# A reciprocal root in one ScalarE operation instead of two, and new paces for the streams of a two-layer trunk

## The chip, the cores and the metric

The kernel runs on one core of a Trainium2 chip. The metric is the device time of one execution in microseconds, the median of several runs.

## What is computed

The reference is a two-layer diffusion-transformer trunk in fp32: 512 latent tokens and 256 context tokens of width 1024. Cut to what matters here:

```python
def rmsnorm(x, g):
    xf = x.astype(jnp.float32)
    y = xf * lax.rsqrt(jnp.mean(xf * xf, axis=-1, keepdims=True) + EPS)
    return (y * g.astype(jnp.float32)).astype(x.dtype)
...
def modulate(x, shift, scale):
    return x * (1 + scale) + shift
...
def swiglu(h, w_gate, w_up, w_down):
    return (jax.nn.silu(h @ w_gate) * (h @ w_up)) @ w_down
```

Each layer is: modulated RMS norm, one input projection, two groups of heads side by side (a gated DeltaNet in both directions with a 64-token chunked triangular solve and a state scan, and multi-head latent attention with an RMS norm on its compressed queries and keys), one output projection, gated residual; then modulated RMS norm, SwiGLU feed-forward, gated residual. A final RMS norm ends it. EPS is 1e-6.

## The kernel before

Activations lie transposed, features on the 128 partitions and tokens along the free axis: a latent tile is 128x512, a context tile 128x256, and 8 of them make the width of 1024. Matrix products split each operand into a high and a low part and make three passes (`gemm`, L215 to L223; the matmul is L222). The helpers record every operation at their own line, so the same few lines recur in the trace: `tt` L140 (tensor with tensor on VectorE), `ts` L144 and L146 (with scalars), `stt` L149 (scalar and tensor), `act` L152 (any ScalarE operation).

**The RMS norm** is `rms_rows`. ScalarE squares the chunks, VectorE sums them, and TensorE adds over the partitions and spreads the sum over all of them (`pc`, L336, in PSUM). Then `q` is −0.5 times the mean plus EPS, `y` a first approximation of the reciprocal root, and one Newton step (Square, `tt`, `stt`) refines it. It is called 15 times: 8 of them 512 wide (latent, with the final one) and 7 of them 256 wide (context). `modulated` calls it ahead of the input projections and the feed-forwards, `mla_norm` for queries and keys, and the last lines of the kernel for the output. Behind it `modulated` scales and shifts eight chunks (VectorE L149, ScalarE into hx or m), and the next matmuls read these.

**The streams.** The program is written as 18 generators, the streams: `ctx_in`, `ctx_chain`, `ctx_mla`, `ctx_ffn`, `ctx_in1` for the context, `lat_in`, `lat_chain` (DeltaNet), `mla_prep`, `mla_att` (attention), `lat_ffn` for the latent tokens, `mod_rest` for the modulation vectors. Each yields now and then how much time it thinks its piece takes. `weave` keeps a clock of its own and always takes up the stream that is due first; a tie goes to the lower rank. The table TUNE gives each stream a rank and a pace, a factor on its yields. So the table decides the order in which the pieces are written into the program, and with it the order in every engine's queue; each engine works its queue off in order. Semaphores do the rest. In the chip no clock of `weave` exists.

Names that come up: the DeltaNet pre-stage (`gdn_pre`) solves 64x64 triangles with 62 small VectorE steps, transposes (L577, L578) and matmuls (L586, L587, L621); the scan's matmuls are L668, L680, L691; the output norm of a DeltaNet block takes its mean by L717, twelve small VectorE steps on 128x8 (`oq`, `ro0y` for the first block, `ro1y` for the second) and a spreading matmul L723. Attention finds row maxima in `prep` (products L932 and L937, reductions L933 and L938), sums in `attend` (L960 scores, L233 values and denominators) and divides by the denominator with the RECIPROCAL of L977. `Mod` multiplies the conditioning vector with the modulation weights (`wmod`, matmuls at L233 into psM, 24 units a layer), and its 256 KB loads go through SP's queue. PSUM tile rings: A has two buffers, M and F one each, B and C two.

Of the kernel before, what the change touches and what calls it, by code (L numbers as in the profile page):

```python
# [14 lines left out]
AF = mybir.ActivationFunctionType  # L15
# [14 lines left out]
EPS = 1e-6  # L30
# [3 lines left out]

C_ID, C_BLK1, C_TRIF, C_TRIB, C_SEL, C_MSK, C_ONE, C_BLKM, C_QB = 0, 128, 256, 384, 512, 520, 524, 525, 527
C_MIN = 529
NCONST = 657
B_MOD, N1, N2, CW, AL, DT, GN, QN, KN, FN = 0, 48, 56, 64, 124, 132, 140, 141, 143, 144
NSMALL = 152

# [9 lines left out]


TUNE = {
    ("ctx_in", 0): (3, 0.876),
    ("ctx_mla", 0): (3, 0.595),
    ("ctx_ffn", 0): (3, 0.702),
    ("ctx_in1", 0): (2, 1.0),
    ("ctx_chain", 0): (0, 0.7),
    ("mod_rest", 0): (1, 0.7),
    ("lat_in", 0): (2, 0.416),
    ("lat_chain", 0): (1, 1.0),  # L60
    ("mla_prep", 0): (4, 1.245),
    ("mla_att", 0): (5, 0.4),
    ("lat_ffn", 0): (6, 1.0),
    ("ctx_chain", 1): (2, 0.85),
    ("mod_rest", 1): (1, 1.0),
    ("lat_in", 1): (1, 0.7),
    ("lat_chain", 1): (0, 0.6),
    ("mla_prep", 1): (5, 1.755),
    ("mla_att", 1): (5, 1.07),
    ("lat_ffn", 1): (6, 1.0),  # L70
}

# [34 lines left out]
def trunk_kernel(ctx, tc, xin, cc, wmod, small, win, wuq, wuk, wuv, wout, wgu, wdn, cst, rope, out):  # L107
# [20 lines left out]
    def slot(tag, dt=F32, w=None):  # L128
        width = WIDTH[tag]
        t = sp.tile([P, width], dt, name=nm(tag), tag=tag, bufs=BUFS[tag])  # L130
        return t[:, 0:w or width]

    def ps(tag):
        return pp.tile([P, 512], F32, name=nm("ps" + tag), tag=tag, bufs=PSB[tag])
# [4 lines left out]
    def tt(out, a, b, op=ALU.mult, e=None):  # L139
        (e or V).tensor_tensor(out=out, in0=a, in1=b, op=op)  # L140

    def ts(out, a, s1, s2=None, op0=ALU.mult, op1=ALU.add, e=None):
        if s2 is None:
            (e or V).tensor_scalar(out=out, in0=a, scalar1=s1, scalar2=None, op0=op0)  # L144
        else:
            (e or V).tensor_scalar(out=out, in0=a, scalar1=s1, scalar2=s2, op0=op0, op1=op1)  # L146

    def stt(out, a, s, b, op0, op1):
        V.scalar_tensor_tensor(out=out, in0=a, scalar=s, in1=b, op0=op0, op1=op1)  # L149

    def act(out, a, f, **kw):
        A.activation(out, a, f, **kw)  # L152
# [7 lines left out]
    nc.sync.dma_start(out=cct, in_=cc)  # L160
    cst_t = cp.tile([P, NCONST], F32, name="cst")
    nc.sync.dma_start(out=cst_t, in_=cst)
# [160 lines left out]
    def rms_rows(st, chunks, scale, tag):  # L323
        n = st.n
        nk = len(chunks)
        pc = ps(tag)[:, 0:n]
        acc = None
        for k, c in enumerate(chunks):
            sq = slot(st.t, w=n)
            act(sq, c, AF.Square)  # L330
            if k and k < nk - 1:
                tt(acc, acc, sq, ADD)
            else:
                acc = sq
            if k >= nk - 2:
                PE.matmul(pc, ones_k.to_broadcast([P, P]), acc, start=k == max(nk - 2, 0), stop=k == nk - 1)  # L336
        q, y, t = (slot(st.t, w=n) for _ in range(3))
        ts(q, pc, -0.5 * scale, -0.5 * EPS)
        act(y, q, AF.Ln, scale=-2.0)
        act(y, y, AF.Exp, scale=-0.5)  # L340
        act(t, y, AF.Square)
        tt(t, t, q)
        stt(y, t, 1.5, y, ADD, MUL)
        return y

    def modulated(st, xs, al, modt, shift, tag, native=False):
        pr = rms_rows(st, xs, 1.0, tag)
        i = st.mi
        hs = []
        if native:  # L350
            for k in range(0, KD, 2):
                t = slot("m")
                for o in (0, 1):
                    h = t[:, NC_ * o:NC_ * o + NC_]
                    stt(h, xs[k + o], al[:, k + o, i:i + 1], pr, MUL, MUL)
                    act(h, h, AF.Identity, bias=modt[:, shift + k + o, i:i + 1])
                    hs.append(h)
            return hs
        for k in range(KD):
            t = slot(st.t, w=st.n)  # L360
            hi, lo = pair(st)
            stt(t, xs[k], al[:, k, i:i + 1], pr, MUL, MUL)
            act(hi, t, AF.Identity, bias=modt[:, shift + k, i:i + 1])
            stt(lo, t, modt[:, shift + k, i:i + 1], hi, ADD, SUB)
            hs.append((hi, lo))
        return hs
# [372 lines left out]
    def mla_norm(l, st, xs, scale, gn, tag):  # L739
        pr = rms_rows(st, xs, scale, tag)  # L740
        res = []
        for k, x_ in enumerate(xs):
            t = slot(st.t, w=st.n)
            stt(t, x_, smalls[l][:, gn + k:gn + k + 1], pr, MUL, MUL)
            if gn == KN and st is CTX:
                kc = sm([P, 2, NC_], "kvc", F32R)
                hi, lo = kc[:, 0, :], kc[:, 1, :]
            else:
                hi, lo = pair(st)
            split(t, hi, lo)  # L750
            res.append((hi, lo))
        return res
# [55 lines left out]
    scale = 96.0 ** -0.5  # L808
# [512 lines left out]
    weave([(TUNE[g.__name__, l][0], paced(g(*a), TUNE[g.__name__, l][1])) for g, l, a in todo])  # L1321
    xx = v.xx
    pr = rms_rows(LAT, xx, 1.0, "A")
    for k in range(KD):
        t = slot("t", w=NL)
# [33 lines left out]
def _constants():  # L1359
    f = np.float32  # L1360
    c = np.zeros((P, NCONST), f)
    p = np.arange(P)
    c[:, C_ID:C_ID + P] = np.eye(P, dtype=f)
    c[:, C_ONE] = 1.0 / D
    same = (p[:, None] // 64) == (p[None, :] // 64)
    c[:, C_BLKM] = (p < 64) / 64.0
    c[:, C_BLKM + 1] = (p >= 64) / 64.0
    c[:, C_BLK1:C_BLK1 + P] = same
    c[:, C_QB] = 64 * EPS * (p < 64)
    c[:, C_QB + 1] = 64 * EPS * (p >= 64)  # L1370
    c[:, C_TRIF:C_TRIF + P] = same & (p[:, None] <= p[None, :])
    c[:, C_TRIB:C_TRIB + P] = same & (p[:, None] >= p[None, :])
    for j in range(4):
        for r in range(2):
            c[32 * j + r, C_SEL + 2 * j + r] = 1.0
    first = (p // 32) % 2 == 0
    c[:, C_MSK] = first
    c[:, C_MSK + 1] = ~first
    c[:, C_MSK + 2] = -1.0 * first
    c[:, C_MSK + 3] = -1.0 * ~first  # L1380
    i = np.arange(64)
    for d, keep in enumerate((i[None, :] >= p[:, None] % 64, i[None, :] <= p[:, None] % 64)):
        c[:, C_MIN + 64 * d:C_MIN + 64 * d + 64] = np.where(keep, 3e38, -1e30)
    t = np.arange(NL)
    inv = f(10000.0) ** (-np.arange(0, 16, 2, dtype=f) / f(16))
    ang = []
    for pos in ((t // GRID_W).astype(f), (t % GRID_W).astype(f)):
        a = pos[:, None] * inv[None, :].astype(f)
        ang += [a, a]
    ang = np.concatenate(ang, axis=1).astype(f)  # L1390
    sign = np.where((np.arange(32) % 16) < 8, -1.0, 1.0).astype(f)
    rope = np.concatenate([np.tile(np.cos(ang).T.astype(f), (4, 1)), np.tile(np.sin(ang).T * sign[:, None], (4, 1))], axis=1)
    return c, rope
# [8 lines left out]
def _layout(i):  # L1402
# [19 lines left out]
    def heads(a):  # L1422
# [7 lines left out]
        [col(i["b_mod"], 48), col(i["norm1_g"], KD), col(i["norm2_g"], KD), cw, heads(i["a_log"]), heads(i["dt_bias"]),  # L1430
         gn, col(i["q_norm_g"], 2), col(i["kv_norm_g"], 1), fn], axis=2)
    o["cst"], o["rope"] = _constants()
    return {k: np.ascontiguousarray(v) for k, v in o.items()}

# [16 lines left out]
```

## Time and profile before

| | |
|---|---|
| median of 3 runs | 2228.44 us (2225.9 to 2229.92) |
| profiled execution, own time | 2224.78 us |
| its span (first to last instruction) | 2223.0 us |
| granted TensorE clock, mean | 0.946 |
| TensorE busy | 2032.2 us, 91% |
| VectorE busy | 1474.6 us, 66% |
| ScalarE busy | 889.5 us, 40% |
| loads of ScalarE tables | 41, 52.6 us |

All rows come from the profiled execution, which is 3.66 us below the median of the runs. The median holds 1.78 us more than the span in that execution (2224.78 less 2223.0). A share of busy time is a mean over stages with different limits; the windows in the section of rows take them apart. Granted clock is a share of TensorE's full speed, 1.00 being full.

### The profile page before, as it was taken

The page shows a single profiled execution, that of the slowest core. Times are in us where ns is not written, and L with a number is a line of the kernel's source. Part 1 is how long each engine was busy: PE and PEld are TensorE (multiplying, and loading weights), DVE is VectorE, ACT ScalarE, POOL GpSimd, SP SyncE. Part 2 cuts the span into 40 slices and gives each one's busy share as a digit, 9 for nine tenths or more (in the row PEclk, how much of TensorE's full clock was granted, in tenths as well). Part 3 has the DMA queues.
Part 4 walks back from the last instruction along what each step waited for, and adds up shares of the span by engine and source line. Part 5 has one row for each costly group of instructions (what it writes and reads, how often), then busy time and mean ns, then how long its engine had stood idle before and what let it go on. Part 6 is the DMA issues. An engine that isn't in the chain of part 4 may idle for free.

```text
span 2223.0 us, 40501 instructions
## 1 busy us (share of the span) xinstructions
PE 2032.2 (91%) x16048; PEld 1591.7 (72%) x16048; DVE 1474.6 (66%) x2904; ACT 889.5 (40%) x1583; POOL 69.6 (3%) x249
## 2 busy tenths in 40 slices
PE   5999988889998899899999998987976989999996
PEld 2876777789995557778888885765644677888885
DVE  4688668876689767769444457887687555444445
ACT  4445365444443534552323234534422234222233
POOL 0000001000000000000000000000000000000000
PEclk8999998899999999999999999996986999999998
DMA  8345514344446202242222236621110022233332
GB/s 327 136 155 188 172 32 124 112 143 132 127 155 208 85 11 80 93 146 91 86 76 96 89 113 221 190 78 29 44 34 11 30 76 76 95 99 96 96 99 76
DMA packets 130638, 240.48 MB, mean 108 GB/s; under 512 B 15185, under 2 KB 30065, under 8 KB 130449
## 3 DMA queue, kind: packets, MB, share of 16 engines
q1 hardware_dynamic: 124592, 224.16, 31.1%
q0 software_dynamic: 5856, 13.74, 2.3%
q8 instruction: 126, 2.06, 0.4%
q14 instruction: 64, 0.52, 0.1%
HBM read 228.30 MB, written 6.91 MB: 106 GB/s over the span
## 4 chain that ended last, share of the span: by engine, by line
PE 76%; DVE 10%; DMA 6%; ACT 5%; issue 3%; SPq 0%; POOL 0%; ACTq 0%; DVEq 0%; POOLq 0%
PE psA L222 35%; PE psM L222 14%; PE psF L222 4%; PE psB L960 3%; PE psA L233 2%; PE psA L227 2%; PE psB L621 2%; PE psM L233 2%; PE psC L668 1%; DVE fl L140 1%; DMA m<-wmod 1%; ACT t L152 1%; DVE g L140 1%; PE psC L680 1%; PE psC L691 1%
## 5 line engine op out<-in xcount | busy, mean ns | idle before, releaser
L222 PE MATMUL psA<-hx,wh 128*128 128x512 f32 x1680 | 537.0, 399 | 24.3 <-ACT hx L152 8.4
L152 ACT ACTIVATE wh<-wr 128x512 fp32r<-128x512 f32 (+2 forms) x410 | 249.1, 608 | 636.4 <-PE psA L222 466.6
L140 DVE TENSOR_TENSOR wl<-wr,wh 128x512 fp32r<-128x512 f32 (+2 forms) x410 | 269.5, 658 | 229.0 <-ACT wh L152 228.4
L222 PEld LDWEIGHTS psA<-hx,wh 128*128 128x128 f32 x1680 | 315.1, 190 | 113.7 <-issue 16.6
L222 PE MATMUL psA<-hx,wl 128*128 128x512 f32 x840 | 330.9, 394 | 1.3 <-DVE wl L140 1.3
L222 PE MATMUL psM<-hx,wh 128*128 128x512 f32 x704 | 217.4, 389 | 0.0
L222 PEld LDWEIGHTS psA<-hx,wl 128*128 128x128 f32 x840 | 159.4, 190 | 36.3 <-DVE wl L140 1.8
L152 ACT ACTIVATE fh<-fr 128x512 fp32r<-128x512 f32 (+3 forms) x186 | 110.7, 599 | 153.8 <-PE psF L222 45.5
L149 DVE SCALAR_TENSOR_TENSOR g<-psA,mod,g 128x512 f32<-128x512 f32 x112 | 83.9, 749 | 104.9 <-PE psA L222 104.6
L222 PEld LDWEIGHTS psM<-hx,wh 128*128 128x128 f32 x704 | 132.2, 188 | 27.2
L140 DVE TENSOR_TENSOR fl<-fr,fh 128x512 fp32r<-128x512 f32 (+3 forms) x186 | 120.0, 648 | 43.3 <-ACT fh L152 39.9
L222 PE MATMUL psM<-hx,wl 128*128 128x512 f32 x352 | 137.0, 389 | 0.0
L222 PE MATMUL psF<-m,fh 128*128 128x256 f32 x600 | 116.3, 292 | 7.1 <-ACT g L152 6.7
L222 PE MATMUL psA<-hd,wh 128*128 128x512 f32 x384 | 120.5, 392 | 0.0
L222 PEld LDWEIGHTS psF<-m,fh 128*128 128x128 f32 x600 | 95.6, 194 | 12.6 <-ACT g L152 9.1
L222 PE MATMUL psA<-ox,wh 128*128 128x512 f32 x320 | 100.7, 393 | 0.0
L222 PE MATMUL psM<-m,fh 128*128 128x256 f32 x416 | 82.1, 295 | 6.9 <-ACT m L152 5.7
L222 PE MATMUL psF<-m,fl 128*128 128x256 f32 x300 | 86.2, 287 | 2.2 <-DVE fl L140 2.1
L222 PEld LDWEIGHTS psA<-hd,wh 128*128 128x128 f32 x384 | 71.7, 188 | 16.4 <-DVE hd L140 1.1
L227 PE MATMUL psA<-m,g 128*128 128x256 f32 x320 | 75.3, 394 | 6.6 <-ACT m L152 3.4
L227 PEld LDWEIGHTS psA<-m,g 128*128 128x128 f32 x320 | 61.8, 197 | 20.3 <-ACT m L152 4.4
L222 PEld LDWEIGHTS psM<-hx,wl 128*128 128x128 f32 x352 | 66.0, 188 | 13.7
(382 smaller groups left out, 3643.0 us busy)
## 6 DMA issues: line engine op xcount, KB each, us to landing
wr<-wgu SPq DMA_DIRECT2D x176, 256.0 KB, 2.6
m<-wmod SPq DMA_DIRECT2D x160, 256.0 KB, 4.0
fr<-wgu SPq DMA_DIRECT2D x88, 256.0 KB, 2.7
wr<-win SPq DMA_DIRECT2D x80, 256.0 KB, 3.3
wr<-wdn SPq DMA_DIRECT2D x64, 256.0 KB, 2.6
g<-win SPq DMA_DIRECT2D x20, 512.0 KB, 6.3
g<-wmod SPq DMA_DIRECT2D x16, 512.0 KB, 10.2
fr<-wdn SPq DMA_DIRECT2D x32, 256.0 KB, 2.7
```

The costliest lines, as they stand in the source:

```text
L140: (e or V).tensor_tensor(out=out, in0=a, in1=b, op=op)
L149: V.scalar_tensor_tensor(out=out, in0=a, scalar=s, in1=b, op0=op0, op1=op1)
L152: A.activation(out, a, f, **kw)
L222: PE.matmul(o, ww[:, wk], xx if n is None else xx[:, a:a + n], start=cnt == 0, stop=cnt == 3 * nk - 1)
L227: PE.matmul(o, w[:, k * P:k * P + P], x_, start=k == 0, stop=k == len(xs) - 1)
L233: prev = mm()
L621: PE.matmul(pv[s, q, d, :], u3(lh[d])[s, c, :], u3(rh[d])[s, c, :], start=True, stop=True)
L668: PE.matmul(o[s], x_[s], y_[s], start=i == 0, stop=i == len(mm) - 1)
L680: PE.matmul(v4(ws)[s, hi, d, :], v4(w)[s, hi, d, :], S[s, hi, d, :], start=True, stop=True)
L691: PE.matmul(v4(kv)[s, hi, d, :], u3(ks[d])[s, unit(hi, n, d), :], v4(u)[s, hi, d, :], start=True, stop=True)
L960: PE.matmul(pst, K[ki][:, b:b + P], Q[qi], start=cnt == 0, stop=cnt == 2)
```

## The change

It has two parts. In `rms_rows` the logarithm and the exponential go, and one ScalarE function, Abs_reciprocal_sqrt, takes their place. It reads `pc` in PSUM directly, with the mean's factor as its scale and EPS as its bias, for which a column is added to the constants. The Newton step stays, and `q` for it too. And in TUNE 13 of 18 entries get other numbers.

```diff
-NCONST = 657
+C_EPS = 657
+NCONST = 658
...
 TUNE = {
-    ("ctx_in", 0): (3, 0.876),
-    ("ctx_mla", 0): (3, 0.595),
...
+    ("ctx_in", 0): (3, 0.815),
+    ("ctx_mla", 0): (0, 0.595),
...
-    ("mla_att", 1): (5, 1.07),
+    ("mla_att", 1): (5, 1.145),
...
         ts(q, pc, -0.5 * scale, -0.5 * EPS)
-        act(y, q, AF.Ln, scale=-2.0)
-        act(y, y, AF.Exp, scale=-0.5)
+        act(y, pc, AF.Abs_reciprocal_sqrt, bias=cst_t[:, C_EPS:C_EPS + 1], scale=scale)
         act(t, y, AF.Square)
         tt(t, t, q)
         stt(y, t, 1.5, y, ADD, MUL)
...
+    c[:, C_EPS] = EPS
```

The lines from the added one to the removed one stand one lower in the changed kernel (`act` is L153, `gemm`'s matmul L223, and so on); from L339 on they stand where they stood. Three places show what becomes of the queues. Loads of ScalarE's tables, which the kernel's text doesn't hold, appear in the order as ACT_TABLE_LOAD.

ScalarE at the end of the program, the final norm (g is the last residual chunk, psA the sum `pc`). Before:

```order
L152 ACTIVATE t_21204<-g_3265_18078 128x512 [waits DVE_49,Activation_49]
L152 ACT_TABLE_LOAD [waits DVE_49]
L152 ACTIVATE t_21208<-t_21207 128x512 [waits Activation_49]
L152 ACT_TABLE_LOAD
L152 ACTIVATE t_21208<-t_21208 128x512 [waits Activation_49]
L152 ACTIVATE t_21209<-t_21208 128x512 [waits PE_49,Activation_49]
```

After, the same place:

```order
L153 ACTIVATE t_21186<-g_3265_18065 128x512 [waits DVE_49,Activation_49]
L153 ACTIVATE t_21190<-g_3265_18065 128x512 [waits DVE_49,Activation_49]
L153 ACT_TABLE_LOAD [waits DVE_49]
L153 ACTIVATE t_21194<-psA_21168,cst 128x512 [waits Activation_49]
L153 ACTIVATE t_21195<-t_21194 128x512 [waits PE_49,Activation_49]
```

One load and one operation are gone; the load that is left waits for VectorE as the first load did.

VectorE at the end of the last triangular solve (small L140 steps on g and st) beside the last head pair's row maxima. Before:

```order
L140 TENSOR_TENSOR st_16899<-g_3095_16888,g_3096_16889 128x31
L140 TENSOR_TENSOR g_3096_16889<-g_3096_16889,st_16899 128x31
L577 STREAM_TRANSPOSE g_3094_16887<-g_3096_16889 128x32x32
L578 STREAM_TRANSPOSE g_3095_16888<-g_3096_16889 128x32x32
L933 TENSOR_REDUCE mx_17210<-psA_17211 128x1
...
L938 TENSOR_REDUCE mx_17210<-psA_17227 128x2
L140 TENSOR_TENSOR m_3175_17231<-mx_17210 128x4
L149 SCALAR_TENSOR_TENSOR g_3020_16504<-psB_17318,cst,g_3020_16504 128x16x32
```

After:

```order
L933 TENSOR_REDUCE mx_17189<-psA_17199 128x1
L141 TENSOR_TENSOR st_16964<-g_3119_16953,g_3120_16954 128x112
L141 TENSOR_TENSOR g_3120_16954<-g_3120_16954,st_16964 128x4x28
L938 TENSOR_REDUCE mx_17189<-psA_17202 128x2
L141 TENSOR_TENSOR st_16964<-g_3119_16953,g_3120_16954 128x87
L141 TENSOR_TENSOR g_3120_16954<-g_3120_16954,st_16964 128x3x29
L938 TENSOR_REDUCE mx_17189<-psA_17206 128x2
...
L141 TENSOR_TENSOR g_3120_16954<-g_3120_16954,st_16964 128x31
L577 STREAM_TRANSPOSE g_3118_16952<-g_3120_16954 128x32x32
L578 STREAM_TRANSPOSE g_3119_16953<-g_3120_16954 128x32x32
```

The six reductions (four L933, two L938) stood behind the transposes and now stand among the steps ahead of them.

VectorE and TensorE at the end of the second layer's attention and DeltaNet output (ro1 is the second block's chain, hx the split rows of the output projection). VectorE before:

```order
L140 TENSOR_TENSOR ro1t_17963<-ro1t_17963,oq_3229_17960 128x8
L977 RECIPROCAL t_18037<-psA_18034 128x512
L149 SCALAR_TENSOR_TENSOR ro1y_17962<-ro1t_17963,ro1y_17962 128x8
L149 SCALAR_TENSOR_TENSOR hd_17680<-t_18037,psA_17681 128x512
L140 TENSOR_TENSOR ro1t_17963<-ro1y_17962 128x8
```

VectorE after:

```order
L977 RECIPROCAL t_18024<-psA_18021 128x512
L141 TENSOR_TENSOR g_2742_14712<-g_2742_14712,psC_17590 128x256
L150 SCALAR_TENSOR_TENSOR hd_17610<-t_18024,psA_17611 128x512
L141 TENSOR_TENSOR g_2719_14594<-g_2719_14594,psC_17590 128x256
L141 TENSOR_TENSOR oq_3225_17852<-psC_17714,qe_16754 128x8
```

TensorE before:

```order
L717 MATMUL psC_17889<-cst,g_3021_16505 128x2 x4
L233 MATMUL psA_17681<-t_18028,m_15984 64x512
L233 MATMUL psA_17681<-t_18022,m_15984 64x512
L233 MATMUL psA_18034<-acc_17692,cst 64x512
L233 MATMUL psA_18034<-acc_17686,cst 64x512
L222 MATMUL psA_18104<-hx_18040,wh_18082 128x512
L222 MATMUL psA_18104<-hx_18041,wh_18082 128x512
L723 MATMUL psC_17889<-cst,ro1y_17962 64x128 x8
```

TensorE after:

```order
L717 MATMUL psC_17892<-cst,g_3025_16508 128x2 x4
L223 MATMUL psA_18129<-hx_18031,wl_18082 128x512
L223 MATMUL psA_18091<-hx_18035,wh_18069 128x512
L223 MATMUL psA_18129<-hx_18035,wh_18081 128x512
L223 MATMUL psA_18091<-hx_18036,wh_18069 128x512
L223 MATMUL psA_18091<-hx_18035,wl_18070 128x512
L223 MATMUL psA_18129<-hx_18036,wh_18081 128x512
L223 MATMUL psA_18129<-hx_18035,wl_18082 128x512
L723 MATMUL psC_17892<-cst,ro1y_17965 64x128 x8
```

The reciprocal moved ahead of the first block's chain (`oq` from psC), and output-projection matmuls of two columns (psA_18091, psA_18129) now stand around L717 and ahead of L723, where the attention's last matmuls stood before.

## Rows read from the trace of the kernel before

**Rows 1.** The page: busy time, share of the span and instructions.

```profile
PE 2032.2 (91%) x16048; PEld 1591.7 (72%) x16048; DVE 1474.6 (66%) x2904; ACT 889.5 (40%) x1583; POOL 69.6 (3%) x249
```

**Rows 2.** Windows: stretch, length, busy us of each engine, granted clock, DMA.

```profile
1495.00:1530.00 35.00, 23.45 (x517) 17.81 (x519) 26.08 (x42) 20.91 (x34) 0.52 (x1) 0.71 0.10 30
1530.00:1640.00 110.00, 93.28 (x1030) 64.06 (x1026) 81.88 (x184) 38.41 (x67) 9.69 (x25) 0.86 0.15 40
1640.00:1784.00 144.00, 113.22 (x1298) 69.45 (x1294) 101.31 (x207) 39.25 (x68) 1.95 (x4) 0.82 0.06 19
...
1850.00:2190.00 340.00, 340.00 (x1497) 279.93 (x1496) 155.25 (x235) 104.09 (x172) 0.00 (x0) 1.00 0.31 97
```

**Rows 3.** Timeline, the final norm: start, us, engine, line, operation.

```profile
2205.33 0.69 DVE L146 TENSOR_SCALAR t<-psA 128x512 f32<-128x512 f32 x1 [1.94 <-PE psA L336]
2206.10 1.28 ACT L152 ACT_TABLE_LOAD   x1 [1.99 <-DVE t L146]
2207.39 0.63 ACT L152 ACTIVATE t<-t 128x512 f32<-128x512 f32 x1
2208.04 1.28 ACT L152 ACT_TABLE_LOAD   x1
```

**Rows 4.** ScalarE's groups by shape: busy us, mean ns of one.

```profile
L152 ACT ACT_TABLE_LOAD x41 | 52.6, 1283 | 9.1 <-DVE t L146 6.0 <-DMA cct<-cc 2.5
...
L152 ACT ACTIVATE t<-t 128x512 f32<-128x512 f32 x33 | 20.7, 628 | 7.3 <-DVE t L149 4.7 <-DVE t L146 2.2
...
L152 ACT ACTIVATE g<-psA,small 128x512 f32<-128x512 f32 x18 | 12.2, 680 | 0.0
...
L152 ACT ACTIVATE tc<-tc 128x256 f32<-128x256 f32 x18 | 7.5, 416 | 2.3 <-DVE tc L146 2.1
```

**Rows 5.** Timeline, TensorE where it starts again behind four norms.

```profile
418.82 1.11 PE L222 MATMUL psM<-m,fh 128*128 128x256 f32 x2 [5.74 <-ACT m L152]
...
907.96 0.64 PE L376 MATMUL psB<-cst,m 32*64 32x16 f32 x16 [3.36 <-ACT m L152]
...
1500.46 0.23 PE L586 MATMUL psB<-g,g 32*32 32x32 f32 x1 [5.56 <-issue]
...
1839.31 0.79 PE L222 MATMUL psA<-hx,wh 128*128 128x512 f32 x1 [8.38 <-ACT hx L152]
```

**Rows 6.** Timeline, the second layer's input norm on ScalarE, and TensorE.

```profile
1349.09 1.39 ACT L152 ACTIVATE hx<-t,mod 128x512 fp32r<-128x512 f32 x2 [2.27 <-DVE t L149]
...
1351.03 1.94 PE L233 MATMUL psM<-m,sc 128*32 128x512 f32 x8 [1.96 <-DMA m<-wmod]
```

**Rows 7.** Timeline, the second layer's tail: VectorE's two chains, and TensorE.

```profile
1767.60 0.17 DVE L140 TENSOR_TENSOR oq<-psC,qe 128x8 f32<-128x8 f32 x1 [3.39 <-PE psC L717]
...
1769.68 0.17 DVE L149 SCALAR_TENSOR_TENSOR ro0y<-ro0t,ro0y 128x8 f32<-128x8 f32 x1
...
1774.52 0.17 DVE L140 TENSOR_TENSOR oq<-psC,qe 128x8 f32<-128x8 f32 x1 [2.01 <-PE psC L717]
...
1777.42 3.36 DVE L977 RECIPROCAL t<-psA 128x512 f32<-128x512 f32 x1
...
1781.81 0.17 DVE L149 SCALAR_TENSOR_TENSOR ro1y<-ro1t,ro1y 128x8 f32<-128x8 f32 x1
...
1780.83 1.22 PE L222 MATMUL psA<-hx,wh 128*128 128x512 f32 x2 [3.46 <-DVE ro1y L149]
```

**Rows 8.** Timeline, the first layer's tail, TensorE.

```profile
854.62 1.22 PE L222 MATMUL psA<-hx,wh 128*128 128x512 f32 x2 [1.21 <-DVE t L977]
```

**Rows 9.** Timeline, VectorE at the last row maxima.

```profile
1707.43 0.69 DVE L933 TENSOR_REDUCE mx<-psA 128x1 f32<-128x512 f32 x1 [1.18 <-PE psA L932]
...
1714.91 0.75 DVE L149 SCALAR_TENSOR_TENSOR g<-psB,cst,g 128x512 f32<-128x512 f32 x1
```

**Rows 10.** L233 in 687–726: matmuls (ns, first and last start), TensorE's idle (us, times).

```profile
L233 PE MATMUL psM<-m,sc x64: 592/605/617, 688.0 to 723.5; 128*32 128x512 f32 x64
...
  DMA m<-wmod: 3.5, 6
```

More of the change, by code (lines that the diff above doesn't have):

```diff
@@ L52 @@
 TUNE = {
-    ("ctx_in", 0): (3, 0.876),
-    ("ctx_mla", 0): (3, 0.595),
-    ("ctx_ffn", 0): (3, 0.702),
+    ("ctx_in", 0): (3, 0.815),
+    ("ctx_mla", 0): (0, 0.595),
+    ("ctx_ffn", 0): (3, 0.751),
     ("ctx_in1", 0): (2, 1.0),
-    ("ctx_chain", 0): (0, 0.7),
-    ("mod_rest", 0): (1, 0.7),
-    ("lat_in", 0): (2, 0.416),
+    ("ctx_chain", 0): (0, 0.651),
+    ("mod_rest", 0): (0, 0.49),
+    ("lat_in", 0): (3, 0.416),
     ("lat_chain", 0): (1, 1.0),
[L61 to L64, printed above, removed]
+    ("mla_prep", 0): (4, 1.332),
+    ("mla_att", 0): (4, 0.17),
+    ("lat_ffn", 0): (6, 0.911),
+    ("ctx_chain", 1): (2, 0.595),
     ("mod_rest", 1): (1, 1.0),
-    ("lat_in", 1): (1, 0.7),
-    ("lat_chain", 1): (0, 0.6),
+    ("lat_in", 1): (2, 0.7),
+    ("lat_chain", 1): (0, 0.642),
     ("mla_prep", 1): (5, 1.755),
-    ("mla_att", 1): (5, 1.07),
+    ("mla_att", 1): (5, 1.145),
     ("lat_ffn", 1): (6, 1.0),
```

## Prediction

> **What bounds the kernel now.** I read the page first, then the windows, then the waits and the timeline. TensorE is busy 2032 of 2223 us and ScalarE 890 [rows 1]: any gain has to come out of the 191 us in which TensorE waits (2223.0 − 2032.2), or out of the slower clock that follows a wait. The windows say where these lie [rows 2]. In 1850–2190, the second layer's feed-forward, TensorE is busy all of the time at a granted clock of 1.00: nothing that ScalarE or an order does there helps. The second layer's latent stage is different: 1495–1530 is busy 23.5 of 35 us at 0.71, 1530–1640 is 93.3 of 110 at 0.86, 1640–1784 is 113.2 of 144 at 0.82, 59 us of waiting in 289. There the chain alternates between TensorE and VectorE, and who stands in front of whom in a queue decides. So the ScalarE edit is priced where a norm stops TensorE, and the pace edit mainly here.
>
> **The ScalarE edit.** Before, a norm issues load, Ln, load, Exp; the final norm shows it: VectorE's scaling at 2205.33, load 2206.10, Ln 2207.39, load 2208.04 for 1.28, then Exp and Square [rows 3]. After, it is one load, one operation that reads PSUM with a pointer for its bias, and Square. The load stays, and so does its place: in the changed order the final load still waits for VectorE, since `ts(q, pc, …)` reads the same PSUM tile first and the new operation comes behind it. Saved are one load and one operation, less what PSUM and the pointer add. No row has this function. The nearest form, a 128x512 from PSUM with a pointer, has 680 ns, against 628 for `t<-t` [rows 4]; I take 680, since the rows show no operation of that shape that differs by its function (bounds 0.63, the plain row, to 1.28, as long as a load). Saving per 512-wide norm: 1.283 + 0.628 − 0.052 = **1.86 us**; per 256-wide norm, with 416 ns: 1.283 + 0.416 − 0.05 = **1.65 us**. For the upper bound of the operation it falls to 1.26.
>
> Fifteen norms have it, but few stand on the path. TensorE waits 8.38 us at the second feed-forward's norm, 3.36 at the second context norm (its gate copies queue behind the first latent feed-forward's norm on ScalarE), 5.74 at the context feed-forward's, 5.56 at the start of the second attention preparation [rows 5]. With the final norm, after which only output follows, that makes four of 512 (final, second feed-forward, first feed-forward, the key norm at 1493) and one of 256: 4 × 1.86 + 1.65 = **9.1 us**. The key norm is the weakest of these: its second load stands on ScalarE between two biased copies that the triangular solve's products wait for, so that without it the second copy comes earlier. Not counted is the second layer's input norm: there hx is ready at 1349.09, and TensorE then still waits 1.96 us for modulation weights until 1351.03 [rows 6]; the DMA is its cover, and without that it would be worth 1.86. The other nine lie beside other streams' matmuls (270–700, and 1340–1495), which is their cover; uncovered they'd be some 15 us more.
>
> The Trainium skill (ScalarE: Activation LUTs, "What ACT_TABLE_LOAD costs") gives a switch 1283 ns and a drain of about 1380 ns more. The trace agrees with the first (1283) and not with the second: Ln starts 0.01 us behind its load [rows 3]. By the page the five counted norms would save 5 × 1.38 = 6.9 us more; the sum goes by the row.
>
> What the edit adds: the new function's table stays, so the next Exp or Tanh on ScalarE needs a load that before was paid inside the norm. In the changed order I count 37 loads against 41, so of the 15 dropped 11 come back elsewhere (I find 12 places, the final norm needs none). They stand ahead of gate, softmax and SwiGLU operations; the one behind the second feed-forward's norm waits for that feed-forward's first matmuls, in a stretch where TensorE has no idle time [rows 2]. I cost them at nothing; each exposed one costs 1.28.
>
> **The pace edit** moves rows on all queues. Three places could be priced.
>
> *Second layer's tail.* The last DeltaNet outputs are normed by twelve small VectorE steps. Undisturbed, the first block takes from 1767.60 to 1769.85; the second takes from 1774.52 to 1781.98, because attention's last 3.36 us reciprocal and two sums stand among its steps, and TensorE's first output-projection matmul at 1780.83, which needs the PSUM tile that the reciprocal reads, waits 3.46 us [rows 7]. In the changed order reciprocal and scaling stand ahead of both chains, and 18 output-projection matmuls ahead of the last products. VectorE still has to do the reciprocal, so its 3.36 us move into the state scan; but TensorE has work then. At most the 3.46 wait and the half clock behind it go (about −6), at least nothing; I take **−3**. The first layer has the same in small, a wait of 1.21 for the reciprocal [rows 8]: **−1** (0 to −1.2).
>
> *Last row maxima.* Before, six reductions of the last head pair stand behind the two transposes of the triangular solve, and each waits about 0.9 us for TensorE, the first at 1707.43; the solve's next step is queued behind them and starts at 1714.91 [rows 9]. In the changed order they stand among the solve's 62 small steps, where their operands come in time or stop the solve. If their products are ready, 1707.43 to 1714.91 goes, plus the first, 9.2 us at most, but six of 0.69 us, 4.1 us, are put ahead of the transposes. Between −9.2 and +4.1 I take **−2**.
>
> Sum: −9.1 − 3 − 1 − 2 = **−15.1**, so the profiled execution of 2224.78 goes to 2209.7. The median shown is 2228.44, 3.7 above that execution, so I forecast **2213 us**.
>
> **Rivals.**
> *Larger gain.* The three places are those I could price, and other queues changed too: if a third of the 59 us in 1495–1784 goes instead of the 5 counted, that is 15 more, **2198**. For it: the clock there is 0.71 to 0.86, so a closed gap also speeds what follows. Against: the same streams with the same data, and VectorE busy most of that stretch, so that its chain can't shrink at will.
>
> *Nothing measurable.* Only norms with nothing beside them pay: final and second feed-forward, 3.7 us, and the orders cancel, **2225**. For it: nine of the fifteen are already covered, and the other three are read from waits that another late operand may end.
>
> *The loads come back on the path.* Twelve returning loads at 1.28 make 15.4 us and cancel the sum: **2228**. For it: they stand right ahead of softmax and gate exponentials, for which TensorE waits. Against: before, the second load of each norm was the same return, on a worse spot. The rule of the Trainium skill that bears on this is in ScalarE: Activation LUTs, "Table sets: the hidden batching unit": every change of set costs a load, and Ln and Exp share one set, so the old pair would need one load and the new function two. The trace differs, since the pair has two loads [rows 3]; that speaks against this rival.
>
> *Slower: a queue behind modulation weights.* Second-layer modulation products, eight groups at 687–724 with one weight transfer each, stand between the first attention's matmuls; they hardly wait now, 3.5 us in six times [rows 10]. In the changed order they stand elsewhere, several with only a few row-maximum products between two groups. TensorE's queue is in order: a group that comes up early stops attention until its transfer lands. The eight groups start 5 us apart (688.0 to 723.5 in seven steps), so one with nothing ahead of it costs up to 5.0. Three exposed take 15 and all of the gain; from four on (20, more than the 15.1 and the 4.5 of a measurable difference) the kernel is slower; with six, 30 − 15.1, it takes **2243**. Against: before, six waits made 3.5 us, 0.6 each, so the transfers keep up as long as attention's pace does.
>
> **How the numbers follow.** Main case 0.50, its own range 2204–2221 (the norms at 1.26 each, or the tail's bounds). Larger gain 0.23. Nothing measurable 0.09 and loads on the path 0.05, together 0.14 for within 0.2%, 4.5 us, about what a measurement here can tell from no change. Slower 0.13. Faster is 0.73. The range 2194–2232 holds the main case, most of the larger gain (below 2194 it would need over half of the 59 us, 0.08) and all without change; above lie the exposed groups, 0.10.
>
> **What would show it.** In the profile after: 37 loads; a final norm with one load and Square about 0.7 us behind the new operation's start, 1.9 us shorter; the wait at the second feed-forward's norm 6.5 instead of 8.4; the reciprocal ahead of the second block's chain, and no 3.5 us wait. The forecast is wrong if the new operation takes much over 0.7, if TensorE waits for modulation weights in the first attention, or if the row maxima stop the solve.

## The result and the profile after

The changed kernel takes 2211.35 us (2208.03 to 2213.97, 4 runs) against 2229.18 of before (4 runs): ratio 0.992, 95% interval [0.9904, 0.9936], that is 17.8 us less (14.3 to 21.4). The forecast was 2213. That it came so near is luck: two of its parts were far off and cancelled, as the experiments show. The ScalarE edit alone is worth 25 us, and the paces take some 7 of them back.

The page after, busy time by engine, as in [rows 1]:

```profile
PE 2033.4 (92%) x16048; PEld 1593.7 (72%) x16048; DVE 1473.7 (67%) x2904; ACT 877.0 (40%) x1564; POOL 69.5 (3%) x249
```

TensorE's work is the same and ScalarE's is 12.5 us less, 5.1 of it loads. ScalarE's groups by shape, which answer to [rows 4] (busy us, mean ns):

```profile
L153 ACT ACT_TABLE_LOAD x37 | 47.5, 1283 | 12.0 <-DVE t L147 6.0 <-DVE tc L147 2.8 <-DMA cct<-cc 2.4
...
L153 ACT ACTIVATE t<-psA,cst 128x512 f32<-128x512 f32 x7 | 4.8, 684 | 0.5 <-DVE t L147 0.5
L153 ACT ACTIVATE tc<-psF,cst 128x256 f32<-128x256 f32 x6 | 2.8, 471 | 3.1 <-DVE tc L147 3.0
```

The new function took 684 ns where 680 were taken. (Two more wide roots, which read psB, stand in a row of their own: the norm runs nine times 512 wide and six times 256 wide, not eight and seven times.) The final norm's timeline, for [rows 3]:

```profile
2195.85 0.69 DVE L147 TENSOR_SCALAR t<-psA 128x512 f32<-128x512 f32 x1 [1.94 <-PE psA L337]
2196.62 1.28 ACT L153 ACT_TABLE_LOAD   x1 [1.99 <-DVE t L147]
2197.92 0.69 ACT L153 ACTIVATE t<-psA,cst 128x512 f32<-128x512 f32 x1
2198.64 0.63 ACT L153 ACTIVATE t<-t 128x512 f32<-128x512 f32 x1
2199.30 0.69 DVE L141 TENSOR_TENSOR t<-t,t 128x512 f32<-128x512 f32 x1 [2.75 <-ACT t L153]
```

In the kernel before, the product behind Square started here:

```profile
2210.66 0.69 DVE L140 TENSOR_TENSOR t<-t,t 128x512 f32<-128x512 f32 x1 [4.64 <-ACT t L152]
```

From the start of VectorE's scaling to that of this product it is 3.45 us now (2199.30 less 2195.85) and was 5.33 (2210.66 less 2205.33): 1.88 less, where 1.86 was worked out. The new function starts 0.02 us behind its load's end, so here too the trace agrees with the 1283 ns of the Trainium skill (ScalarE: Activation LUTs, "What ACT_TABLE_LOAD costs") and shows none of the 1380 ns drain on top.

TensorE behind the four norms of [rows 5]:

```profile
414.06 1.13 PE L223 MATMUL psM<-m,fh 128*128 128x256 f32 x2 [5.38 <-ACT m L153]
...
902.57 0.65 PE L376 MATMUL psB<-cst,m 32*64 32x16 f32 x16 [1.48 <-ACT m L153]
...
1490.92 0.23 PE L586 MATMUL psB<-g,g 32*32 32x32 f32 x1 [7.12 <-issue]
...
1829.64 0.80 PE L223 MATMUL psA<-hx,wh 128*128 128x512 f32 x1 [6.50 <-ACT hx L153]
```

Two fell by 1.88 as forecast (8.38 to 6.50, 3.36 to 1.48). The context feed-forward's fell by 0.36, and the key norm's rose by 1.56. The end of the second transpose on VectorE (L578), first before, then in the changed kernel, shows what ended the key norm's wait:

```profile
1498.43 1.93 DVE L578 STREAM_TRANSPOSE g<-g 128x1024 f32<-128x1024 f32 x1
```

```profile
1488.89 1.93 DVE L578 STREAM_TRANSPOSE g<-g 128x1024 f32<-128x1024 f32 x1
```

In both traces the waiting products start 0.10 us behind that end (1500.46 behind 1500.36, 1490.92 behind 1490.82), so the norm was not what ended that wait. At the context feed-forward's norm it is the product behind Square on VectorE, first before, then in the changed kernel with Square ahead of it:

```profile
416.53 0.43 DVE L140 TENSOR_TENSOR tc<-tc,tc 128x256 f32<-128x256 f32 x1 [1.12 <-ACT tc L152]
```

```profile
409.91 0.42 ACT L153 ACTIVATE tc<-tc 128x256 f32<-128x256 f32 x1
...
411.75 0.42 DVE L141 TENSOR_TENSOR tc<-tc,tc 128x256 f32<-128x256 f32 x1
```

Before, VectorE waited for ScalarE here. Now Square ends at 410.33, and VectorE gets to the product 1.42 us later, since small steps of the triangular solve stand ahead of it: what ScalarE saved, the product waits in VectorE's queue.

The windows of the second layer's latent stage, for [rows 2] (same stages, the start of each found by the stage's first matmuls):

```profile
1482.80:1519.00 36.20, 23.77 (x465) 16.36 (x464) 27.07 (x48) 16.55 (x29) 0.52 (x1) 0.72 0.12 38
1519.00:1629.00 110.00, 97.05 (x1089) 66.96 (x1085) 86.36 (x190) 43.08 (x75) 9.48 (x25) 0.91 0.16 42
1629.00:1776.70 147.70, 113.37 (x1305) 69.87 (x1304) 98.56 (x204) 37.48 (x64) 1.95 (x4) 0.82 0.06 17
```

The three stages last 293.9 us; before, from 1494.0 to 1784.0, 290.0. Before, a group of modulation products stood between the latent input and the stage's start at 1494; counted from the last matmul of the latent input, with 2851 matmuls in both, it is 293.8 and 292.9. Here the forecast took 6.9 off (key norm, tail, row maxima); on equal work the profile shows 0.9 more. The tail, for [rows 7]:

```profile
1756.84 3.36 DVE L977 RECIPROCAL t<-psA 128x512 f32<-128x512 f32 x1 [0.37 <-PE psA L234]
...
1772.78 0.17 DVE L141 TENSOR_TENSOR oq<-psC,qe 128x8 f32<-128x8 f32 x1 [2.17 <-PE psC L717]
...
1775.34 0.17 DVE L150 SCALAR_TENSOR_TENSOR ro1y<-ro1t,ro1y 128x8 f32<-128x8 f32 x1
...
1760.26 0.73 PE L223 MATMUL psA<-hx,wh 128*128 128x512 f32 x2 [2.03 <-DVE t L977]
...
1775.56 1.09 PE L723 MATMUL psC<-cst,ro1y 128*64 128x128 f32 x16 [0.77 <-DVE ro1y L150]
1778.89 1.23 PE L223 MATMUL psA<-hx,wh 128*128 128x512 f32 x3 [2.24 <-ACT hx L153]
```

What was said of the order came true. The second block's chain takes 2.7 us instead of 7.5. But the reciprocal now delays the state scan ahead of it (2.03), and the output projection, which has started early, comes to the rows of the second block 2.24 too soon: 5.0 us of waits in place of 4.3 (3.46 and one of 0.87). The first layer's tail, for [rows 8], does the same in small: the wait for the reciprocal (1.21) is gone, and one for the second block's rows stands there:

```profile
854.87 1.55 PE L223 MATMUL psA<-hx,wh 128*128 128x512 f32 x3 [1.54 <-ACT hx L153]
```

The row maxima, for [rows 9]:

```profile
1689.72 0.69 DVE L933 TENSOR_REDUCE mx<-psA 128x1 f32<-128x512 f32 x1 [0.37 <-PE psA L932]
...
1697.62 0.69 DVE L938 TENSOR_REDUCE mx<-psA 128x2 f32<-128x512 f32 x1 [0.45 <-PE psA L937]
...
1699.18 1.92 DVE L577 STREAM_TRANSPOSE g<-g 128x1024 f32<-128x1024 f32 x1
```

Each of the six waits for its product, 0.26 to 0.45 (before, five of the six did, 0.89 to 1.18), now in front of the solve's last steps. The transpose behind the solve, in the kernel before:

```profile
1701.96 1.94 DVE L577 STREAM_TRANSPOSE g<-g 128x1024 f32<-128x1024 f32 x1
```

From the last matmul of the latent input to this transpose's end it was 212.8 us and is now 218.2 (1701.10 less 1482.9); from there to the last of L723 it was 80.1 and is 75.6. The stage lost ahead of the transposes what it won behind them.

At the first attention, TensorE's waits for modulation weights, for [rows 10] (us, times):

```profile
  DMA m<-wmod: 4.1, 3
```

The slower rival did not come: 3.5 us in six waits became 4.1 in three, the longest 2.62, and the stage as a whole got shorter. This table gives the last matmul of a stream in each trace, as its difference to before in us (the last line is the span); the runs are those of the next section.

| last matmul of | before | changed | ars_only | tune_only | five_norms | ten_norms | old_layer2 |
|---|---|---|---|---|---|---|---|
| latent input, layer 0 | 267.9 | −5.2 | −7.4 | +2.9 | −0.7 | −4.1 | −3.4 |
| context feed-forward | 684.7 | −0.6 | −7.0 | +10.5 | −1.3 | −4.5 | −4.3 |
| first attention | 851.2 | −9.3 | −7.9 | +1.5 | +1.5 | −7.7 | −14.4 |
| latent feed-forward, layer 0 | 1338.5 | −7.6 | −10.9 | +6.1 | −3.0 | −10.5 | −9.9 |
| latent input, layer 1 | 1491.1 | −8.2 | −10.8 | +7.3 | −2.7 | −11.2 | −11.0 |
| latent DeltaNet, layer 1 | 1784.0 | −7.3 | −10.4 | +10.7 | +1.3 | −7.4 | −15.1 |
| latent feed-forward, layer 1 | 2202.4 | −9.5 | −12.9 | +9.6 | −1.3 | −7.7 | −17.7 |
| span | 2223.0 | −11.1 | −14.8 | +9.4 | −3.2 | −7.6 | −19.8 |

A profiled execution is one draw. That of before lies 4 us under its median, that of `ars_only` 7 above its own, so the table places gains and losses between stages and is no measure of the sum. A second execution of `ars_only` (`root_only_again`, below) differs from the first by up to 2.7 us in it.

### The profile page after: what moved, and what is told of

It reads as the page before. It is cut to its first block, busy times and chain, and to the rows that moved or that the text cites. A ratio compares the mean times of both kernels' runs of the same rounds, so it can differ in the third digit from the quotient of the medians.

```text
span 2211.9 us, 40502 instructions
## 1 busy us (share of the span) xinstructions
PE 2033.4 (92%) x16048; PEld 1593.7 (72%) x16048; DVE 1473.7 (67%) x2904; ACT 877.0 (40%) x1564; POOL 69.5 (3%) x249
## 5 line engine op out<-in xcount | busy, mean ns | idle before, releaser
L223 PE MATMUL psA<-hx,wh 128*128 128x512 f32 x1680 | 541.0, 401 | 21.7 <-ACT hx L153 12.4
L153 ACT ACTIVATE wh<-wr 128x512 fp32r<-128x512 f32 (+2 forms) x410 | 248.9, 608 | 651.4 <-PE psA L223 462.2
L223 PEld LDWEIGHTS psA<-hx,wh 128*128 128x128 f32 x1680 | 317.6, 192 | 112.3 <-ACT hx L153 15.7
L223 PE MATMUL psA<-hx,wl 128*128 128x512 f32 x840 | 334.1, 398 | 0.0
L223 PE MATMUL psM<-hx,wh 128*128 128x512 f32 x704 | 218.2, 390 | 0.0
L223 PEld LDWEIGHTS psA<-hx,wl 128*128 128x128 f32 x840 | 161.1, 192 | 37.7 <-issue 0.8
L153 ACT ACTIVATE fh<-fr 128x512 fp32r<-128x512 f32 (+3 forms) x186 | 110.6, 600 | 148.1 <-PE psM L223 41.2
L223 PEld LDWEIGHTS psM<-hx,wh 128*128 128x128 f32 x704 | 132.6, 189 | 27.4
L223 PE MATMUL psM<-hx,wl 128*128 128x512 f32 x352 | 137.0, 389 | 0.0
L223 PE MATMUL psF<-m,fh 128*128 128x256 f32 x600 | 115.5, 291 | 7.5 <-ACT g L153 6.8
L223 PE MATMUL psA<-hd,wh 128*128 128x512 f32 x384 | 120.5, 392 | 0.0
L223 PEld LDWEIGHTS psF<-m,fh 128*128 128x128 f32 x600 | 94.8, 193 | 14.3 <-ACT g L153 8.3
L223 PE MATMUL psA<-ox,wh 128*128 128x512 f32 x320 | 100.7, 393 | 0.0
L223 PE MATMUL psF<-m,fl 128*128 128x256 f32 x300 | 85.9, 286 | 1.3 <-DVE fl L141 1.3
L223 PE MATMUL psM<-m,fh 128*128 128x256 f32 x416 | 81.2, 293 | 5.9 <-ACT m L153 5.4
L223 PEld LDWEIGHTS psA<-hd,wh 128*128 128x128 f32 x384 | 71.7, 188 | 16.5 <-DVE hd L141 1.1
L153 ACT ACTIVATE t<-psB 128x512 f32<-128x512 f32 x80 | 47.6, 597 | 72.5 <-PE psB L960 50.0
L223 PEld LDWEIGHTS psM<-hx,wl 128*128 128x128 f32 x352 | 66.2, 188 | 13.7
```

Of the source, the lines that this page charges most:

```text
L223: PE.matmul(o, ww[:, wk], xx if n is None else xx[:, a:a + n], start=cnt == 0, stop=cnt == 3 * nk - 1)
```

## The experiments

Theory A is the prediction's: five norms are on the path, and the order gives 6 us more. The rivals: B, that only the two norms with nothing beside them pay and the order does the rest; C, that the ten norms costed at nothing are paid for too. Medians in us; the ratio is to before, run beside each.

| run | median | ratio [95% interval] |
|---|---|---|
| the changed kernel | 2211.35 | 0.992 [0.9904, 0.9936] |
| ars_only | 2202.82 | 0.9888 [0.9872, 0.9905] |
| tune_only | 2232.5 | 1.0018 [1.0001, 1.0034] |
| root_first | 2210.41 | 0.9918 [0.9896, 0.994] |
| old_layer2 | 2207.14 | 0.9906 [0.9893, 0.9919] |
| five_norms | 2222.47 | 0.9972 [0.996, 0.9983] |
| ten_norms | 2217.18 | 0.9943 [0.993, 0.9955] |
| root_att0_paces | 2206.16 | 0.9885 [0.9869, 0.9901] |
| root_first_old_paces | 2195.09 | 0.9843 [0.9825, 0.986] |
| load_back | 2220.97 | 0.9953 [0.9935, 0.9971] |
| ctx_paces | 2206.91 | 0.9901 [0.9886, 0.9916] |
| no_newton | 2185.02 | 0.9804 [0.9788, 0.9821] |

**The two parts alone.** `ars_only` has the ScalarE edit and TUNE of before; `tune_only` the reverse, with logarithm and exponential:

```diff
-        act(y, q, AF.Ln, scale=-2.0)
-        act(y, y, AF.Exp, scale=-0.5)
+        act(y, pc, AF.Abs_reciprocal_sqrt, bias=cst_t[:, C_EPS:C_EPS + 1], scale=scale)
```

> Only the ScalarE edit; TUNE as before. Theory A (the prediction's terms): five norms on the path give 9.1 us, so about 2220 against 2229. Theory B (only norms with nothing beside them pay, that is the final one and the second feed-forward's, and the order does the rest): 3.7 us, about 2225.5. Both expect the final norm, from VectorE's scaling to the first output product, 1.9 us shorter.

> Only the pace edit; logarithm and exponential stay. Theory A: the order gives 6 us, so about 2223. Theory B: the order gives what theory B's norms don't, 17.8 - 3.7 = 14, so about 2215. If the two edits add up, this gain and that of the ScalarE edit alone make 17.8 us.

Both theories missed both. The ScalarE edit gives 25 us (21 to 29), the paces cost 4 (0.2 to 7.6). Added, −21 lies within the noise of the measured −17.8.

**Which norms.** `five_norms` has the new function where the prediction counted it and the old pair elsewhere; `ten_norms` is the counterpart. Each caller passes the flag `one`:

```diff
-        act(y, pc, AF.Abs_reciprocal_sqrt, bias=cst_t[:, C_EPS:C_EPS + 1], scale=scale)
+        if one:
+            act(y, pc, AF.Abs_reciprocal_sqrt, bias=cst_t[:, C_EPS:C_EPS + 1], scale=scale)
+        else:
+            act(y, q, AF.Ln, scale=-2.0)
+            act(y, y, AF.Exp, scale=-0.5)
```

> TUNE as before; the new function only in the five norms that the prediction counted (context feed-forward, both latent feed-forwards, the second layer's key norm, the final one), logarithm and exponential in the other ten. Theory A (the five carry the gain): 9.1 us off 2229, so 2220, and the ten carry the rest only through the order. Theory C (the other ten, most of them in the first 400 us, are on the path too): also about 2220, but then the ten alone give the missing 17 us.

> The counterpart: the new function only in the other ten norms, TUNE as before. Theory A: they lie beside other work, 2229 less 0 to 2. Theory C: 15 to 17 us less, 2212 to 2214; in the trace the first 270 us come out about 7 us shorter, as they did with all fifteen.

The five give 6.2 us (3.8 to 8.9), a little less than the 9.1. The ten give 12.7 (10.0 to 15.6), twice as much, and they were costed at nothing; theory C wanted 15 to 17. The table of stages says where the ten gain: 4.1 up to 268, 3.2 in the first attention, 2.8 in the feed-forward behind it; 3.8 are lost again between 1491 and 1784. Five and ten together make 18.9, some 6 less than the 25 of all fifteen; the intervals overlap, and no run says what those 6 are. ScalarE in the kernel before, in the stretch of the context's query and key norms:

```profile
189.47 0.68 ACT L152 ACTIVATE t<-psA,small 128x512 f32<-128x512 f32 x1
190.16 1.28 ACT L152 ACT_TABLE_LOAD   x1
191.46 0.42 ACT L152 ACTIVATE tc<-tc 128x256 f32<-128x256 f32 x1
191.78 0.62 ACT L152 ACTIVATE wh<-wr 128x512 fp32r<-128x512 f32 x1
192.42 1.28 ACT L152 ACT_TABLE_LOAD   x1
193.71 0.87 ACT L152 ACTIVATE tc<-tc 128x256 f32<-128x256 f32 x2
...
196.78 0.70 ACT L152 ACTIVATE tc<-m 128x256 f32<-128x256 f32 x2
...
197.23 1.13 PE L336 MATMUL psF<-tc,cst 128*128 128x256 f32 x4 [1.96 <-ACT tc L152]
```

and the same place in `ars_only`:

```profile
188.11 1.28 ACT L153 ACT_TABLE_LOAD   x1 [1.83 <-DVE t L150]
...
190.25 0.71 ACT L153 ACTIVATE tc<-m 128x256 f32<-128x256 f32 x2
...
190.71 1.13 PE L337 MATMUL psF<-tc,cst 128*128 128x256 f32 x4 [0.33 <-ACT tc L153]
```

ScalarE hardly idles here (15.99 of 18 us below), whatever its 40% over the span. A load doesn't only delay its own norm: the next norm's squares (tc<-m) and the weight splits (wh<-wr), on which other streams' matmuls wait, stand behind it in the one queue. Windows of 188 to 206, first before, then `ars_only`:

```profile
188.00:206.00 18.00, 16.05 (x77) 12.05 (x76) 15.36 (x33) 15.99 (x27) 0.71 (x3) 1.00 0.25 87
```

```profile
188.00:206.00 18.00, 17.67 (x88) 12.95 (x81) 16.96 (x38) 15.13 (x27) 1.71 (x7) 1.00 0.51 164
```

TensorE, busy 16.05 of 18 us before, gets 17.67. The windows are the same stretch of time and not quite the same work, since `ars_only` is some us ahead here; the wait of 1.96 that became 0.33 is the closer comparison.

**The load by itself.** `load_back` is `ars_only` with a 128x1 exponential behind the root, which brings the load back into the norm:

```diff
         act(y, pc, AF.Abs_reciprocal_sqrt, bias=cst_t[:, C_EPS:C_EPS + 1], scale=scale)
+        act(t[:, 0:1], y[:, 0:1], AF.Exp)
```

> The ScalarE edit with TUNE as before, and right behind the root a 128x1 exponential into a column that Square overwrites: it forces the table load that the edit took out of the norm, and little else. If the gain of 26 us is the load inside the norm (theory C, all fifteen norms count with 1.28 of their 1.7 to 1.9 us), most of it goes: 2203 + 15 x (1.28 + 0.2) = 2225 at most, 2218 to 2225. If it is the shorter chain of wide operations or the order alone that helped: 2203 to 2208.

18 us come back by the medians (14.5 by the ratios), of 25, some of it the added operation itself (201 ns, fifteen times). So the load in that place is likely most of the gain; it is not shown apart from the order, since over 270 of VectorE's 2904 instructions stand elsewhere in its queue than in `ars_only`. It is not a smaller count of loads: `ars_only` has 39 in its order, before 41, `load_back` 42. Thirteen of the fifteen loads that left the norms came back, ahead of gates and exponentials. They seem to cost little there: in the trace of `ars_only` one of them, at 899.3, is followed within 2.5 us by a wait of TensorE for ScalarE, of 0.85.

**The chain of the norm.** Two kernels shorten it with TUNE of before; the first issues the root ahead of VectorE's scaling, the second leaves out the Newton step too, and with it the scaling, so that its root is only as exact as the new function:

```diff
-        ts(q, pc, -0.5 * scale, -0.5 * EPS)
         act(y, pc, AF.Abs_reciprocal_sqrt, bias=cst_t[:, C_EPS:C_EPS + 1], scale=scale)
+        ts(q, pc, -0.5 * scale, -0.5 * EPS)
```

> The ScalarE edit with TUNE as before, and the root issued ahead of VectorE's scaling of the same tile. Theory A: 0.8 to 2.0 us for each exposed norm, for five norms 4 to 10 below 2203, so 2193 to 2199. If the scaling is hidden but at the second feed-forward and the final norm: 2199 to 2201.

> TUNE as before and the root first, but without the Newton step: scaling, Square, product and last step are left out, so the root is only as exact as the new function. On the final norm's chain that is 2.1 us (Square 0.63, product and step 0.69 each, gaps). Theory C (each of the fifteen norms is paid in full or nearly, as 24 to 28 us for fifteen times 1.65 to 1.86 say): 2195 less 15 x 2.1 x 0.8 to 1.0, 2164 to 2170. Theory A (five pay, the rest lie beside other work): 2195 less 5 x 2.1, 2184 to 2186.

The first takes 7.7 us off `ars_only` by the medians, as theory A has it, and is the fastest version that keeps the Newton step: it beats before by 35 us and the changed kernel by 16. Its final norm:

```profile
2179.91 1.28 ACT L153 ACT_TABLE_LOAD   x1
2179.94 1.12 PE L337 MATMUL psA<-t,cst 128*128 128x512 f32 x2 [0.26 <-ACT t L153]
2181.20 0.69 ACT L153 ACTIVATE t<-psA,cst 128x512 f32<-128x512 f32 x1
2181.92 0.63 ACT L153 ACTIVATE t<-t 128x512 f32<-128x512 f32 x1
2181.92 0.69 DVE L147 TENSOR_SCALAR t<-psA 128x512 f32<-128x512 f32 x1 [2.76 <-ACT t L153]
```

The load runs beside the last sum's matmul, and the root starts 0.14 us behind that matmul's end; in the changed kernel 2.11 pass, since scaling and load come in between. `no_newton` takes another 10.1 (8.7 by the ratios): five times 2.1, theory A, and not fifteen times. Which norms pay, its total doesn't say. By the traces it is no further than `root_first_old_paces` at the second layer's latent input, and then wins 1.8 us up to the end of the DeltaNet, 2.8 up to that of the feed-forward and 2.7 behind it. Read together, and as far as the order lets one read it: of a norm's latency few norms are paid; of its load, more of them.

**The paces.** `old_layer2` is the changed kernel with four entries of before, `ctx_paces` and `root_att0_paces` are `ars_only` with six (context input, attention, feed-forward and chain, modulation and latent input of the first layer) and three of the new ones. Two of the edits, cut:

```diff
 # old_layer2
-    ("ctx_chain", 1): (2, 0.595),
+    ("ctx_chain", 1): (2, 0.85),
...
-    ("lat_in", 1): (2, 0.7),
-    ("lat_chain", 1): (0, 0.642),
+    ("lat_in", 1): (1, 0.7),
+    ("lat_chain", 1): (0, 0.6),
...
-    ("mla_att", 1): (5, 1.145),
+    ("mla_att", 1): (5, 1.07),
 # root_att0_paces
-    ("mla_prep", 0): (4, 1.245),
-    ("mla_att", 0): (5, 0.4),
-    ("lat_ffn", 0): (6, 1.0),
+    ("mla_prep", 0): (4, 1.332),
+    ("mla_att", 0): (4, 0.17),
+    ("lat_ffn", 0): (6, 0.911),
```

> The changed kernel with the four second-layer paces of before (context chain, latent input, latent chain, attention). Theory A: the second layer's tail and row maxima give their 5 us back, 2216. Theory B, as the trace after reads (the stage from 1494 to 1784 of before is 3.7 us longer in the changed kernel, and the gain lies in the first layer's attention): the same or up to 4 us faster, 2208 to 2211.

> The ScalarE edit with only the six new paces of the context stage (context input, attention, feed-forward, chain; modulation and latent input of the first layer). If they carry the loss up to 685 us that the trace after shows (the context feed-forward's norm sums behind the latent chain's transposes on VectorE), 2203 + 4 to 6, so 2207 to 2209, and with the second layer's four paces (4 us) that explains the 2211 of the changed kernel. If the loss comes only from paces together: 2203.

> The ScalarE edit with only three of the new paces (first layer's attention preparation, attention, feed-forward). If the order's gain lies in the first layer's attention (that stage was 8 us shorter in the trace after) and its loss in the context paces: 2203 less up to 8, so 2195 to 2203. If the three paces cost like the rest: 2203 to 2208.

Against their neighbours these are 3 to 4 us each by the medians and 3, 3 and none by the ratios, and the intervals overlap, so none of them is shown by itself. `old_layer2` is 4.2 under the changed kernel, and its trace puts the gain into the second layer: from the latent input's end to the feed-forward's end it wins 6.7 us on before, the changed kernel 1.3. But what the four paces alone do there depends on the rest. In the second layer's latent stage `old_layer2` has the same instructions as `ars_only` in the same order on TensorE, VectorE, ScalarE and GpSimd (by the names in the traces). First `ars_only`, then `old_layer2`:

```profile
1480.30:1773.60 293.30, 235.64 (x2852) 154.22 (x2851) 212.69 (x446) 97.89 (x169) 12.03 (x30) 0.82 0.10 29
```

```profile
1480.10:1768.90 288.80, 230.86 (x2852) 151.02 (x2851) 212.61 (x446) 97.88 (x169) 12.02 (x30) 0.84 0.10 30
```

The one order takes 293.3 us at a granted clock of 0.82 and 288.8 at 0.84. `root_only_again` and `root_att0_paces` have it too and are with the first (293.0 and 293.4, 0.82); `ctx_paces`, which shares the new context paces with `old_layer2`, is with the second (288.9, 0.84). The changed kernel's order takes 293.8 at 0.84. So the four new paces lose 5.0 us in this stage against the one time that the old order has, and 0.5 against the other; what ahead of the stage decides between the two stays open.

`ctx_paces` is 4.1 over `ars_only` by the medians. In its trace it has lost 3.0 us to `ars_only` at the context feed-forward's end and wins 4.4 in the stage just shown. The row behind that loss, VectorE and TensorE at the context feed-forward's norm in the changed kernel:

```profile
400.24 0.42 DVE L141 TENSOR_TENSOR tc<-tc,tc 128x256 f32<-128x256 f32 x1
400.57 0.70 DVE L565 STREAM_TRANSPOSE g<-st 128x512 f32<-128x512 f32 x1
...
401.56 1.94 DVE L567 STREAM_TRANSPOSE g<-g 128x1024 f32<-128x1024 f32 x1
403.44 0.37 DVE L141 TENSOR_TENSOR tc<-tc,tc 128x256 f32<-128x256 f32 x1
...
406.61 2.07 PE L337 MATMUL psF<-tc,cst 128*128 128x256 f32 x4 [4.43 <-DVE tc L141]
```

The latent chain's transposes stand among the norm's sums, and TensorE waits 4.43 for them (4.65 in the trace of `ctx_paces`). In `ars_only` L567 runs at 395.06, ahead of most of the sums, and TensorE's longest wait at these matmuls (L337) is 0.82. `root_att0_paces` shows no gain over `ars_only`: by its trace the first attention ends 5.9 us earlier (13.8 against 7.9 ahead of before), and the feed-forward behind it ends at the same place, 10.9 ahead. What attention gains is work put off: its stage has 1353 matmuls in 159.4 us where `ars_only` has 1495 in 165.6, and the next stage 3132 in 490.2 where that has 2986 in 484.3, with TensorE busy for 98% of it.

**Root first under the new paces, and a second look.**

> The changed kernel with the reciprocal root issued ahead of VectorE's scaling of the same PSUM tile. ScalarE then waits for TensorE alone, and its table load stands ahead of that wait. Theory A (norms on the path): the scaling (0.69 and a gap of 0.08) leaves the path, and the load (1.28) too where ScalarE is free before the sum is ready, as at the final norm: 0.8 to 2.0 us for each of five norms, 4 to 10 us, so 2201 to 2207. Theory B: two norms, 1.5 to 4 us, 2207 to 2210. If the scaling was hidden anyway: 2211.

> The ScalarE edit alone once more, for a second profile: its first was taken in its longest execution (2210 against a median of 2203). If single executions differ in the first 300 us, where most transfers run (237 GB/s in the first 100 us of before), the two traces part there and run alike behind it; if not, they part in the stages that wait for one another, 1494 to 1784.

`root_first` gives 0.9 us, against 7.7 under the old paces; its six runs go from 2198 to 2217, so that nothing follows but that the gain is not safe there. `root_only_again` took 2212.1, and its trace parts from the first by up to 2.7 us between 300 and 760 and runs alike elsewhere, so neither of the two expectations held.

## Why the prediction was right, and where it was not

- **The operation.** Right: 684 ns for 680, and 1.88 us for 1.86 at the final norm and at two of the waits.
- **The five norms, 9.1 us.** 6.2 measured (3.8 to 8.9). Three were as said. The key norm's wait had another end (the transposes), and the context feed-forward's saving went into a wait of its next product in VectorE's queue.
- **"The other nine lie beside other streams' matmuls, which is their cover."** This step failed; with the second layer's input norm, costed at nothing too, ten norms bring 12.7. TensorE's work beside a norm seems to cover the norm's latency (`no_newton`), but not its load: in the rows at 188 to 206 that holds up the queue from which the cover itself, the split weights and other squares, is fed, and `load_back` agrees. The prediction read the norms' waits from TensorE and ScalarE's load from its mean over the span, 40%. It also placed the nine wrongly: in the trace before, two of them lie in the stretches that it names (loads at 277.7 and 310.0), four lie in the first 270 us (10.9, 97.8, 190.2, 199.6), of which it shows no row of ScalarE, and three at 751, 967 and 1507.
- **The pace edit, −6.** The second failure, with the wrong sign: +4 alone, 7 to 8.5 on top of the ScalarE edit. For the three places the term was read from a wait that would go. At each it did go or move, and others took its place: the reciprocal in the scan, the output projection ahead of its rows in both layers (2.24 and 1.54), the maxima ahead of the solve. The context feed-forward's norm, with its 4.43 us, wasn't looked at. And one and the same order takes 288.8 or 293.3 us in the second layer's latent stage, at a granted clock of 0.84 or 0.82, so that terms of 1 to 3 us there could not be read from the waits alone.
- **Returning loads.** Right as far as seen: they cost little. By the Trainium skill (ScalarE: Activation LUTs, "Table sets: the hidden batching unit") Ln followed by Exp needs one load. This case's traces differ: each pair had two, and with the pair gone the count fell from 41 to 39 (`ars_only`) and 37.
- **Modulation weights.** Right: in the first attention TensorE's waits for them stayed small, 4.1 us for 3.5.
- **Two readings.** Of the six row maxima the first, at 1705.60, did not wait; five did. And for 2194 some 24 of the 59 us would have to go (19 more than the forecast's, and the 5 counted), which is 0.4 and not over half.

What stays open: the profiled executions of `ars_only` took 2210 and 2212 while its four plain ones took 2199 to 2203, so some 10 of its 25 us stand in no trace; why the root ahead of the scaling pays only under the old paces; what sets the granted clock of the second layer's latent stage; and how much of the ten norms' gain is the order. TUNE does not fix the order alone: it is the same in before and `ars_only`, and yet over 200 of VectorE's 2904 instructions stand elsewhere in its queue. In `ars_only` a group of first-layer modulation products, for which TensorE waited 2.12 us at 115, came 12 us later without that wait; in `root_first_old_paces` a group stayed in that place, with a wait of 0.54, and that kernel is faster still.

## What to carry to other kernels

Here a table load held up the streams that feed through ScalarE, so price one by what is queued behind it in that stretch, and not by the engine's mean load. A reader of PSUM that can start an engine's longer chain is worth trying ahead of the one that only needs its value later. When one of two edits is an order tuned by numbers, run each alone: here the sum hid a gain of 25 and a loss of 7. And before a few us of a stage are put down to its order, compare its granted clock in both traces.

## What was not expected of the hardware

Root and scaling read the same PSUM tile, on two engines, and the second waits for the first by the program's order; swapping them let the load run beside the matmul (0.14 us from sum to root for 2.11). Five executions of four kernels ran the same instructions in the same order through the second layer's latent stage, and took 293.0 to 293.4 us (three, granted clock 0.82) or 288.8 and 288.9 (two, 0.84). And one kernel's executions differ more than another's: 2198 to 2217 for `root_first`, 2206.1 to 2208.6 for `ctx_paces`.
